# Attention steps spread over a slot, splits at the slot's begin, sample products on GpSimd

## The chip, the cores and the metric

The kernel runs on one core of one Trainium2 chip. Time is device microseconds of one execution; the program is launched once and computes everything in that launch. TensorE is called PE, VectorE DVE, ScalarE ACT, GpSimd POOL and SyncE SP, as in the profile. PEld is the loading of stationary operands on PE.

## The reference, cut to what matters

One layer of a decoder, for a prompt of 2048 tokens and 8 x 4 sample tokens, all in float32. Changed is the scheduling of the first part, the projection and the attention over the prompt:

```python
qa, ka, va, qb, kb, vb, ga, gb = _project(x, w_in)          # one product x @ w_in
qa, ka, qb, kb = _rope(qa, pos), _rope(ka, pos), _rope(qb, pos), _rope(kb, pos)
# A: window of 128, 8 query heads, 2 key heads, a learned sink per head
s = _band_scores(qa.reshape(n, t, A_KV_HEADS, A_GROUP, HEAD_DIM), ka, A_WINDOW)
p = _sink_softmax(s, _sink_logits(sink_a))
oa = _band_values(p, va).reshape(n, t, A_Q)
# B: three groups of 4 heads, (window, dilation) = (128, 1), (512, 4), (2048, 16)
for g, (win, dil) in enumerate(B_DIL):
    qg, kg, vg = (_stride_split(z[:, :, hs], dil) for z in (qb, kb, vb))
    s = _band_scores(qg[:, :, :, None], kg, win // dil)
    p, lse = _softmax_lse(s)
    outs.append(...)                                         # p @ v
```

The scores of a block of 128 queries go against its own block of keys and, where there is one, the block before. The sample tokens attend to caches; the scores of B's sample tokens are sums of products of a query row with cached key rows. After the attention come gates, projections, a layer norm and a gated convolutional FFN, which the change does not touch.

## The kernel before

**Precision.** Every operand of a large product is split into a high and a low half (float32r): `split` copies the high half on ACT and subtracts on DVE (on POOL where it is told so) to get the low half. A product is then three matmuls: high x high, low x high, high x low.

**Slots.** Phase 1 is a row of slots. A slot projects one block of 128 tokens (or the 32 sample tokens) with four units of 256 columns of the weights of its kind. The kinds come in this order: B0, B1, B2 (the three groups of B: q, k, v and a quarter of the gates), A (q, k, v and a part of the gates), G (the rest of the gates). Each has 16 prompt slots; a sample slot, called 16, follows them (in G it comes after the third). A prompt slot is 4 units x 8 k-blocks x 3 = 96 matmuls of 256 columns into two PSUM tiles `psd` (half 0: units 0 and 1, half 1: units 2 and 3; two buffers, so half 0 of the next slot uses the tile of half 0 of this one). The tokens of a slot, `xs`, are split from the transposed input `R` by `make_xs`, one slot ahead; B1 reads R with a stride of 4 tokens, B2 with a stride of 16.

**Steps.** Between groups of 12 matmuls (unit u, half kh of its k-blocks, so eight places a slot, (0, 0) to (3, 1)) `slot` calls `adv`, which advances every attention job by one step (up to its next `yield`). A job is a generator, `attn_b` or `attn_a`, made at a slot's end and advanced through the next slot and into the one after. The order in which Python emits instructions is the order on each engine's queue: an engine takes its instructions strictly in that order, and an instruction that waits holds all those behind it. At (1, 0) and one more place `adv_bg` advances `sample_scores`, which for each pair of sample tokens loads 128 cached keys and the query rows (SP), multiplies them (L797) and sums by head (L800). It gives up four places first, then does 16 pairs: this falls in slots 2 to 9 of B1 and of B2 (two pairs a slot) and 2 to 13 of A (two a slot up to slot 5, then one).

**Evacuation.** When half 0 of psd is complete, `evac` applies the rotary embedding on DVE (`rope`: product with the cosines, product of the swapped halves with the sines, L425 and L426, sum L433); it is emitted at the place `evac_at`. Half 1 is evacuated at the slot's end: the gate's part is copied by ACT (L449); in B the v part stays in PSUM until `split_v` in the job's second step; in A, v is split at once.

**A job of B** transposes q and k (PE), splits them (`split_q`, `split_k`: ACT high, DVE low), computes the scores (`qk`, eight matmuls), and runs the softmax: row maxima with the mask on DVE (L546), minus the scaled maximum `nm` (L550), exponential with the row sum on ACT (L552). P is transposed (PE, L562) and split (`transpose_p`), and multiplied by the values (L659). `both` adds the two halves of the result (ACT L570, DVE L571); POOL adds the parts of two halves (L662) and issues the store (L663). **A job of A** does the same twice, for two head pairs r = 0 and 1 of each key head, with the sink as one more column of P (L693, L695, L698, L700), and stores with two DMAs on POOL (L718).

`bufp` is a ring of ten 2 KB-wide buffers for loads and temporaries. PSUM pools: pd 2 tiles, psS 2 (scores), psT 3 (transposes, and the second of B's value tiles), psO 1.

Of the kernel before, what the change touches and what calls it, by code (L numbers as in the profile page):

```python
# [7 lines left out]
F32 = mybir.dt.float32  # L8
F32R = mybir.dt.float32r
AF = mybir.ActivationFunctionType  # L10
ALU = mybir.AluOpType
# [6 lines left out]
NS = 32  # L18
# [16 lines left out]
class Net:  # L35
# [142 lines left out]
    def phase1(self):  # L178
        nc, tc, a = self.nc, self.tc, self.a
        with ExitStack() as st:  # L180
# [39 lines left out]
            self.jobs = []  # L220
            self.vprev = None
            sa = ExitStack()
            for n, (kind, i, t) in enumerate(seq):
# [16 lines left out]
                def prep():  # L240
# [10 lines left out]
                    if t[0] == "p" and nextp:  # L251
                        return self.make_xs(nextp[0][2], kind == "A")
# [37 lines left out]
    def adv(self):  # L290
        for j in self.jobs[::-1]:
            try:
                next(j)
            except StopIteration:
                self.jobs.remove(j)

# [55 lines left out]
    def slot(self, kind, i, t, xs, units, prep, after_unit, rp):  # L352
# [5 lines left out]
        evac_at = (2, 1) if kind[0] == "B" else (2, 0)  # L358
# [5 lines left out]
        if kind == "A" and i == 16:  # L364
            pace = (0, 0, 1, 1, 1, 1, 2, 2)
        for half in range(2):
            ps = self.pd.tile([128, 512], F32, tag="d", name="psd")
            for uu in range(2):
# [20 lines left out]
                if u == (1 if kind[0] == "B" and i == 0 else 0):  # L389
                    out = prep()  # L390
                    if kind == "G" and i == 14:
                        rp.close()
                        self.phase2_weights()
# [59 lines left out]
    def evac(self, kind, i, t, half, ps):  # L453
# [37 lines left out]
    def evac_sample(self, kind, half, ps):  # L491
# [9 lines left out]
        if half == 0:  # L501
            self.cs_s = self.at.tile([NS, 128], F32, tag="cs", name="css")
            nc.sync.dma_start(self.cs_s, a["c_rope"][rows, :])
            q = self.at1.tile([NS, 512], F32, tag="q", name="sq")
# [36 lines left out]
    def softmax_pair(self, sps, nk, mask, m, nm, den, cols, accum=True, init=None):  # L541
# [8 lines left out]
        nc.vector.tensor_scalar(nm[:, csl], m[:, csl], -SCALE, None, ALU.mult)  # L550
# [71 lines left out]
    def attn_b(self, kind, i, t):  # L622
# [6 lines left out]
        for p in range(2):  # L629
            nc.tensor.transpose(ps[:, p * 128:(p + 1) * 128], q[:, p * 128:(p + 1) * 128], self.idn)  # L630
        qT = self.split_q(ps[:, 0:256].rearrange("p (r t) -> p r t", r=2))
        ps = self.psO.tile([128, 512], F32, tag="o", name="pst")
        for p in range(2):
            nc.tensor.transpose(ps[:, p * 128:(p + 1) * 128], kv[:, p * 128:(p + 1) * 128], self.idn)
# [3 lines left out]
        vprev, self.vprev = self.vprev, v  # L638
        yield
# [4 lines left out]
        nc.gpsimd.dma_start(self.d_md[g, rows, :], md)  # L644
        yield
        vs = [v] if nb == 1 else ([v, vprev] if swap else [vprev, v])
        PTs = []
# [4 lines left out]
        O = self.buf()  # L652
        for x in range(2):
            yield
            ops = self.psT.tile([128, 512], F32, tag="t", name="pso") if x else self.psO.tile([128, 512], F32, tag="o", name="pso")
            for c in range(2):
                for b in range(nb):
                    k = (c * nb + b) * 128
                    nc.tensor.matmul(ops[:, c * 256:(c + 1) * 256], lhsT=vs[b][c][:, x].rearrange("p s d -> p (s d)"),  # L659
                                     rhs=PTs[x][:, :, k:k + 128], start=(b == 0), stop=(b == nb - 1))  # L660
            o = self.both(O, ops, x).rearrange("p (c s t) -> p c s t", c=2, s=2)
# [4 lines left out]
    def attn_a(self, t):  # L666
# [15 lines left out]
        yield  # L682
        m = self.at.tile([128, 8], F32, tag="m8", name="m8")
# [5 lines left out]
        def softmax(r, x, sps):  # L689
# [8 lines left out]
            nc.vector.tensor_scalar(nm[:, c:c + 2], m[:, c:c + 2], -SCALE, None, ALU.mult)  # L698
# [11 lines left out]
        def values(r, x, PT):  # L710
            for b in range(nb):
                for q in range(2):
                    nc.tensor.matmul(ops[:, r * 256:(r + 1) * 256], lhsT=vs[b][:, x], rhs=PT[:, q, b * 256:(b + 1) * 256],
                                     start=(b == 0 and q == 0), stop=(b == nb - 1 and q == 1))

        def out(x):
            o = self.both(O, ops, x)
            nc.gpsimd.dma_start(self.d_oa[x * 256:(x + 1) * 256, rows].rearrange("(h d) t -> d h t", h=4),  # L718
                                o.rearrange("p (h t) -> p h t", h=4))

        sps = scores(0)
        P0, P1 = softmax(0, 0, sps), softmax(0, 1, sps)
        yield
        yield
        t0 = trans(P0)
        sps = scores(1)
        P0 = softmax(1, 0, sps)
        yield
        ops = self.psO.tile([128, 512], F32, tag="o", name="pso")
        values(0, 0, t0)  # L730
        yield
        t0 = trans(P0)
        yield
        P0 = softmax(1, 1, sps)
        yield
        values(1, 0, t0)
        O = self.buf()
        out(0)
        t0 = trans(P1)
        yield  # L740
        t1 = trans(P0)
        yield
        ops = self.psO.tile([128, 512], F32, tag="o", name="pso")
        values(0, 1, t0)
        yield
        values(1, 1, t1)
        out(1)
# [18 lines left out]
    def sample_scores(self, g):  # L766
# [25 lines left out]
        for n, (b, th) in enumerate(steps):  # L792
# [4 lines left out]
            nc.vector.tensor_tensor(q3, Kv, q3, ALU.mult)  # L797
# [835 lines left out]
```

## Time and profile before

| | us |
|---|---|
| median of 3 runs | 3260.72 |
| lowest, highest | 3258.58, 3261.48 |
| the profiled execution | 3259.99 |
| its span, first to last instruction | 3258.2 |
| mean granted clock of TensorE | 0.994 |
| PE busy in the span | 3175.0 |
| DVE busy in the span | 1947.6 |

The span is what the profile shows, and the execution's own time is 1.8 us longer. Phase 1 takes the first 1300 us or so. There the load of the other engines differs from place to place; this is the view that gives each engine's busy time in stretches of 100 us (us of the stretch, then busy us and instructions of each engine, the granted clock, the DMA share and GB/s):

```profile
100.00:200.00 100.00, 100.00 (x856) 99.72 (x856) 62.25 (x164) 61.39 (x155) 17.74 (x26) 1.00 0.17 54
300.00:400.00 100.00, 94.79 (x784) 91.71 (x783) 79.98 (x196) 58.85 (x145) 17.54 (x26) 1.00 0.25 71
600.00:700.00 100.00, 96.80 (x811) 94.57 (x810) 80.23 (x205) 60.28 (x160) 22.70 (x35) 1.00 0.33 99
900.00:1000.00 100.00, 98.27 (x786) 92.55 (x785) 80.11 (x205) 62.37 (x187) 19.11 (x17) 1.00 0.20 50
```

The engines stand in the order PE, PEld, DVE, ACT, POOL. The first stretch lies in B0, the second in B1, the third in B2, the fourth in A. In the rows of groups a line gives: line of the kernel, engine, operation, tiles written and read, shape, count, then busy us in all, mean ns of one, and the idle time of the engine before it with what ended it. In the rows of waits the numbers are us in all, times, and the longest.

### The profile page before, as it was taken

The page shows a single profiled execution, that of the slowest core. Times are in us where ns is not written, and L with a number is a line of the kernel's source. Part 1 is how long each engine was busy: PE and PEld are TensorE (multiplying, and loading weights), DVE is VectorE, ACT ScalarE, POOL GpSimd, SP SyncE. Part 2 cuts the span into 40 slices and gives each one's busy share as a digit, 9 for nine tenths or more (in the row PEclk, how much of TensorE's full clock was granted, in tenths as well). Part 3 has the DMA queues.
Part 4 walks back from the last instruction along what each step waited for, and adds up shares of the span by engine and source line. Part 5 has one row for each costly group of instructions (what it writes and reads, how often), then busy time and mean ns, then how long its engine had stood idle before and what let it go on. Part 6 is the DMA issues. An engine that isn't in the chain of part 4 may idle for free.

```text
span 3258.2 us, 56718 instructions
## 1 busy us (share of the span) xinstructions
PE 3175.0 (97%) x21839; PEld 2907.4 (89%) x21839; DVE 1947.6 (60%) x4030; ACT 1397.0 (43%) x3097; POOL 565.5 (17%) x671
## 2 busy tenths in 40 slices
PE   8999999999999899899999999999999999999999
PEld 8998999999899899788877988888888888999998
DVE  5667877877887632577765444564446444574446
ACT  6666656665666533412224243342243332342332
POOL 2112112223121200255540000030002100030001
PEclk9999999999999999999999999999999999999999
DMA  3113212412221343876744323443334423443231
GB/s 116 56 47 95 82 31 86 121 63 89 79 57 38 91 131 98 227 194 175 187 131 140 121 84 101 127 142 91 95 100 120 139 86 101 120 138 91 69 95 57
DMA packets 480036, 343.02 MB, mean 105 GB/s; under 512 B 113938, under 2 KB 435564, under 8 KB 479766
## 3 DMA queue, kind: packets, MB, share of 16 engines
q1 hardware_dynamic: 462390, 290.78, 31.5%
q0 software_dynamic: 17232, 48.56, 4.8%
q8 instruction: 172, 2.82, 0.4%
q14 instruction: 98, 0.80, 0.1%
q10 hardware_dynamic: 144, 0.07, 0.0%
HBM read 279.71 MB, written 59.59 MB: 104 GB/s over the span
## 4 chain that ended last, share of the span: by engine, by line
PE 58%; issue 2%; DMA 2%; DVE 1%; SPq 0%; ACT 0%; POOL 0%; DVEq 0%; POOLq 0%; ACTq 0%
PE psu L1392 31%; PE psdn L1070 14%; PE psw L1070 5%; PE psb L1070 4%; PE psd L379 2%; PE psdf L1070 1%; DMA oa<-d_oa 1%; PE pst L1234 0%; PE pso L964 0%; PE pst L1269 0%; DMA ob<-d_ob 0%; DMA ga<-d_gate 0%; DMA b<-in_w_o 0%; SPq L1126 0%; DMA b<-in_w_br_b 0%
## 5 line engine op out<-in xcount | busy, mean ns | idle before, releaser
L1392 PE MATMUL psu<-h,w 128*128 128x512 f32 (+1 forms) x5280 | 1013.6, 354 | 2.2 <-ACT h L41 2.0
L379 PE MATMUL psd<-w,xs 128*128 128x256 f32 x7680 | 1001.1, 285 | 8.7 <-ACT w L41 4.0
L1392 PEld LDWEIGHTS psu<-h,w 128*128 128x128 f32 x5280 | 861.2, 188 | 149.0 <-ACT h L41 3.4
L379 PEld LDWEIGHTS psd<-w,xs 128*128 128x128 f32 x7680 | 945.7, 190 | 12.9 <-ACT w L41 4.4
L1070 PE MATMUL psdn<-w,gt 128*128 128x256 f32 (+1 forms) x4008 | 474.9, 279 | 2.2 <-DVE y L1443 2.2
L1070 PEld LDWEIGHTS psdn<-w,gt 128*128 128x128 f32 (+1 forms) x4008 | 472.2, 186 | 5.3 <-DVE y L1443 4.5
L42 DVE TENSOR_TENSOR w<-b,w 128x512 fp32r<-128x512 f32 (+1 forms) x613 | 403.7, 717 | 21.4 <-ACT w L41 20.4
L41 ACT ACTIVATE w<-b 128x512 fp32r<-128x512 f32 x636 | 346.5, 607 | 127.4 <-PE psdn L1070 64.2
L1403 ACT ACTIVATE ext<-psu 128x512 f32<-128x512 f32 (+1 forms) x110 | 56.3, 512 | 452.2 <-PE psu L1392 452.1
L1416 DVE SCALAR_TENSOR_TENSOR ac<-ext,cw,ac 128x512 f32<-128x512 f32 (+1 forms) x88 | 71.1, 808 | 286.9 <-ACT ac L1415 286.9
L1443 DVE SCALAR_TENSOR_TENSOR y<-y,psdn 128x256 f32<-128x256 f32 x176 | 73.2, 420 | 274.2 <-PE psdn L1070 270.4
L1070 PE MATMUL psw<-WO,mT 128*128 128x512 f32 (+1 forms) x800 | 189.4, 395 | 0.9 <-DVE mT L42 0.9
L1070 PEld LDWEIGHTS psw<-WO,mT 128*128 128x128 f32 (+1 forms) x800 | 148.5, 186 | 38.9 <-DVE mT L42 1.1
L1412 POOL COPY mix<-ext 128x2 f32<-128x2 f32 x66 | 13.0, 196 | 926.5 <-ACT ext L1403 906.4
L42 DVE TENSOR_TENSOR xs<-R,xs 128x1024 fp32r<-128x1024 f32 x64 | 104.8, 1638 | 114.9 <-ACT xs L41 114.8
L1070 PE MATMUL psb<-w,oT 128*128 128x512 f32 (+1 forms) x600 | 147.6, 404 | 7.7 <-ACT b L449 5.0
L41 ACT ACTIVATE gt<-ac 128x512 fp32r<-128x512 f32 x110 | 58.3, 549 | 222.2 <-DVE ac L1423 162.7
L1070 PEld LDWEIGHTS psb<-w,oT 128*128 128x128 f32 (+1 forms) x600 | 112.4, 190 | 36.3 <-ACT b L449 5.7
L552 ACT ACTIVATE P<-P,nm 128x256 f32<-128x256 f32 (+1 forms) x192 | 86.4, 451 | 123.1 <-issue 87.4
L42 DVE TENSOR_TENSOR PT<-pst,PT 128x512 fp32r<-128x512 f32 (+1 forms) x160 | 96.2, 608 | 66.6 <-ACT PT L41 66.0
L662 POOL TENSOR_TENSOR b<-b 64x256 f32<-64x256 f32 x96 | 71.3, 742 | 337.4 <-DVE b L571 337.4
L41 ACT ACTIVATE xs<-R 128x1024 fp32r<-128x1024 f32 x80 | 116.2, 1452 | 0.9 <-ACT b L756 0.4
(257 smaller groups left out, 3679.1 us busy)
## 6 DMA issues: line engine op xcount, KB each, us to landing
b<-in_w_up SPq DMA_DIRECT2D x352, 256.0 KB, 3.9
b<-in_w_down SPq DMA_DIRECT2D x160, 256.0 KB, 3.4
b<-in_w_in SPq DMA_DIRECT2D x80, 256.0 KB, 4.1
b<-in_x_prompt SPq DMA_DIRECT2D x64, 256.0 KB, 4.0
b<-in_cache_b SPq DMA_DIRECT2D x64, 256.0 KB, 3.3
ga<-d_gate SPq DMA_DIRECT2D x32, 512.0 KB, 5.4
b<-d_q SPq DMA_DIRECT2D x48, 256.0 KB, 3.9
d_gate<-b SPq DMA_DIRECT2D x64, 128.0 KB, 1.9
```

Of the source, the lines that this page charges most:

```text
L41: self.nc.scalar.activation(hi, src, AF.Copy)
L42: (eng or self.nc.vector).tensor_tensor(lo, src, hi.bitcast(F32), ALU.subtract)
L379: nc.tensor.matmul(dst, lhsT=l, rhs=r[:, k, :], start=(k == 0 and q == 0), stop=(k == 7 and q == len(ops) - 1))
L552: nc.scalar.activation(P[:, x, :nk], P[:, x, :nk], AF.Exp, bias=nm[:, c:c + 1], scale=SCALE, accum_out=den[:, c:c + 1])
L662: nc.gpsimd.tensor_tensor(o[:, :, 0], o[:, :, 0], o[:, :, 1], ALU.add)
L1070: self.nc.tensor.matmul(ps[:x.shape[1]], lhsT=x, rhs=w, start=(first and q == 0), stop=(last and q == len(ops) - 1))
L1392: nc.tensor.matmul(ps[:, :b1 - b0], lhsT=w[:, k, c0:c0 + 128], rhs=h[:, x, k, b0:b1], start=(k == 0 and q == 0), stop=(k == 7 and q == 2))
L1403: nc.scalar.activation(ext[:, 2 + b0:2 + e1], ps[:, 0:e1 - b0], AF.Copy)
L1412: nc.gpsimd.tensor_copy(carry[:, j, :], ext[:, W:W + 2])
L1416: nc.vector.scalar_tensor_tensor(ac[:, :L], ext[:, 1:1 + L], cw[:, 1, j:j + 1], ac[:, :L], ALU.mult, ALU.add)
L1443: nc.vector.scalar_tensor_tensor(y[x][:M, cs], y[x][:M, cs], ALPHA if first else 1.0, ps[:M], ALU.mult, ALU.add)
```

## The change

- **Jobs.** `adv` goes through the jobs from the oldest to the newest (before, the reverse), and then runs what was put on the list `late`.
- **B.** q and k are transposed into one PSUM tile, in one go. The values are split one step later; the scores come one step later. The two transposes of P, before in two separate steps of the same slot, both come at the first place of the next slot, directly ahead of the newer job's transposes. Both value products come together two steps after that, and their sums and store are run from `late`.
- **A.** The scores of r = 0 come one step later with both softmaxes; two steps on both P tiles are transposed, and the scores and both softmaxes of r = 1 follow at once; its transposes come at the first place of the next slot. The values of each r go into one PSUM tile, and each r is stored with two DMAs.
- **xs.** `prep` (loads, the transposes of x in B0, and `make_xs`) is called at the slot's begin, except in B0's first slot. The low half is computed by POOL in B1, B2 and A (before in A alone).
- **rope.** q and k of B lie side by side in one tile, and the rotary embedding takes three DVE instructions for five. Half 0 is evacuated at (2, 0) in B too (before (2, 1)).
- **nm** is computed by ACT.
- **Sample scores.** The product (L797) is done by POOL; the sum stays on DVE.

```diff
     def adv(self):
-        for j in self.jobs[::-1]:
+        for j in list(self.jobs):
             try:
                 next(j)
             except StopIteration:
                 self.jobs.remove(j)
+        while self.late:
+            self.late.pop()()
...
-                        return self.make_xs(nextp[0][2], kind == "A")
+                        return self.make_xs(nextp[0][2], kind != "B0" and kind != "G")
...
-        evac_at = (2, 1) if kind[0] == "B" else (2, 0)
+        evac_at = (2, 0)
...
+        if kind != "B0" or i > 0:
+            out = prep()
...
-            q = self.at1.tile([128, 512], F32, tag="q", name="q")
-            kv = self.at1.tile([128, 512], F32, tag="kv", name="kv")
-            self.q, self.kv = q, kv
+            t = self.at1.tile([128, 1024], F32, tag="qkv", name="qkv")
+            q = t[:, 0:512] if kind == "A" else t[:, 256:512]
+            self.q, self.kv = q, t[:, 512:1024]
...
-                self.rope([(q[:, 0:256].rearrange("p (h d) -> p h d", d=64), 0, 4),
-                           (kv[:, 0:256].rearrange("p (h d) -> p h d", d=64), 4, 8)], ps, cs, 128, 8)
+                self.rope([(t[:, 256:768].rearrange("p (h d) -> p h d", d=64), 0, 8)], ps, cs, 128, 8)
...
-        nc.vector.tensor_scalar(nm[:, csl], m[:, csl], -SCALE, None, ALU.mult)
+        nc.scalar.activation(nm[:, csl], m[:, csl], AF.Copy, scale=-SCALE)
...
 # attn_b
-        for p in range(2):
-            nc.tensor.transpose(ps[:, p * 128:(p + 1) * 128], q[:, p * 128:(p + 1) * 128], self.idn)
+        for p in range(4):
+            nc.tensor.transpose(ps[:, p * 128:(p + 1) * 128], (q, kv)[p // 2][:, p % 2 * 128:(p % 2 + 1) * 128], self.idn)
         qT = self.split_q(ps[:, 0:256].rearrange("p (r t) -> p r t", r=2))
-        ps = self.psO.tile([128, 512], F32, tag="o", name="pst")
-        for p in range(2):
-            nc.tensor.transpose(ps[:, p * 128:(p + 1) * 128], kv[:, p * 128:(p + 1) * 128], self.idn)
-        self.split_k(ps[:, 0:256].rearrange("p (r t) -> p r t", r=2), i % 2)
+        self.split_k(ps[:, 256:512].rearrange("p (r t) -> p r t", r=2), i % 2)
+        yield
         yield
         v = self.split_v(self.vps)
...
         nc.gpsimd.dma_start(self.d_md[g, rows, :], md)
-        yield
...
+        for _ in range(5):
+            yield
+        PTs = [self.transpose_p(P, [(c, b) for c in range(2) for b in range(nb)]) for P in Ps]
+        yield
+        yield
+        tiles = []
         for x in range(2):
-            yield
-            PTs.append(self.transpose_p(Ps[x], [(c, b) for c in range(2) for b in range(nb)]))
...
+        self.late.append(lambda: self.sum_b(g, i, tiles))
+
+    def sum_b(self, g, i, tiles):
+        nc = self.nc
+        O = self.buf()
+        for x, ops in enumerate(tiles):
             o = self.both(O, ops, x).rearrange("p (c s t) -> p c s t", c=2, s=2)
             nc.gpsimd.tensor_tensor(o[:, :, 0], o[:, :, 0], o[:, :, 1], ALU.add)
         nc.gpsimd.dma_start(self.d_ob[g]...)
...
 # attn_a
+        def values(r, PTs):
+            ops = self.psO.tile([128, 512], F32, tag="o", name="pso")
+            for x in range(2):
+                for b in range(nb):
+                    for q in range(2):
+                        nc.tensor.matmul(ops[:, x * 256:(x + 1) * 256], lhsT=vs[b][:, x],
+                                         rhs=PTs[x][:, q, b * 256:(b + 1) * 256],
+                                         start=(b == 0 and q == 0), stop=(b == nb - 1 and q == 1))
+            o = self.both(self.buf(), ops, r)
+            for x in range(2):
+                h0 = (4 * x + 2 * r) * 64
+                nc.gpsimd.dma_start(self.d_oa[h0:h0 + 128, rows].rearrange("(y d) t -> d y t", y=2),
+                                    o[:, x * 256:(x + 1) * 256].rearrange("p (y t) -> p y t", y=2))
...
         sps = scores(0)
+        Ps = [softmax(0, x, sps) for x in range(2)]
+        yield
+        yield
+        PTs = [trans(P) for P in Ps]
         sps = scores(1)
+        Ps = [softmax(1, x, sps) for x in range(2)]
+        yield
+        yield
+        values(0, PTs)
+        yield
+        PTs = [trans(P) for P in Ps]
+        yield
+        yield
+        values(1, PTs)
...
 # sample_scores
-            nc.vector.tensor_tensor(q3, Kv, q3, ALU.mult)
+            nc.gpsimd.tensor_tensor(q3, Kv, q3, ALU.mult)
```

More of the change, by code (lines that the diff above doesn't have):

```diff
@@ L219, in phase1 @@
             units += [self.next_unit(pool=True) for _ in range(2)]
-            self.jobs = []
+            self.jobs, self.late = [], []
             self.vprev = None
@@ L388, in slot @@
                         self.adv_bg()
-                if u == (1 if kind[0] == "B" and i == 0 else 0):
+                if u == 1 and kind == "B0" and i == 0:
                     out = prep()
-                    if kind == "G" and i == 14:
-                        rp.close()
-                        self.phase2_weights()
+                if u == 0 and kind == "G" and i == 14:
+                    rp.close()
+                    self.phase2_weights()
                 after_unit(u)
@@ L503, in evac_sample @@
             nc.sync.dma_start(self.cs_s, a["c_rope"][rows, :])
-            q = self.at1.tile([NS, 512], F32, tag="q", name="sq")
+            q = self.at1.tile([NS, 1024], F32, tag="qkv", name="sq")[:, 0:512]
             kv = self.buf(NS)
@@ L638, in attn_b @@
         vprev, self.vprev = self.vprev, v
+        vs = [v] if nb == 1 else ([v, vprev] if swap else [vprev, v])
         yield
@@ L644, in attn_b @@
         nc.gpsimd.dma_start(self.d_md[g, rows, :], md)
+        for _ in range(5):
+            yield
+        PTs = [self.transpose_p(P, [(c, b) for c in range(2) for b in range(nb)]) for P in Ps]
         yield
-        vs = [v] if nb == 1 else ([v, vprev] if swap else [vprev, v])
-        PTs = []
         yield
+        tiles = []
         for x in range(2):
-            yield
-            PTs.append(self.transpose_p(Ps[x], [(c, b) for c in range(2) for b in range(nb)]))
-        O = self.buf()
-        for x in range(2):
-            yield
             ops = self.psT.tile([128, 512], F32, tag="t", name="pso") if x else self.psO.tile([128, 512], F32, tag="o", name="pso")
+            tiles.append(ops)
             for c in range(2):
@@ L697, in softmax @@
                                                accum_out=m[:, c + y:c + y + 1])
-            nc.vector.tensor_scalar(nm[:, c:c + 2], m[:, c:c + 2], -SCALE, None, ALU.mult)
+            nc.scalar.activation(nm[:, c:c + 2], m[:, c:c + 2], AF.Copy, scale=-SCALE)
             for y in range(2):
@@ L708, in trans @@
             return self.transpose_p(P, [(y, b) for b in range(nb) for y in range(2)])
[L710 to L719, printed above, removed]
+        def values(r, PTs):
[11 more added lines that the diff above has]
+                                    o[:, x * 256:(x + 1) * 256].rearrange("p (y t) -> p y t", y=2))
@@ L721, in attn_a @@
         sps = scores(0)
-        P0, P1 = softmax(0, 0, sps), softmax(0, 1, sps)
+        Ps = [softmax(0, x, sps) for x in range(2)]
         yield
         yield
-        t0 = trans(P0)
+        PTs = [trans(P) for P in Ps]
         sps = scores(1)
-        P0 = softmax(1, 0, sps)
+        Ps = [softmax(1, x, sps) for x in range(2)]
         yield
-        ops = self.psO.tile([128, 512], F32, tag="o", name="pso")
-        values(0, 0, t0)
         yield
-        t0 = trans(P0)
+        values(0, PTs)
@@ L733, in attn_a @@
         yield
-        P0 = softmax(1, 1, sps)
+        PTs = [trans(P) for P in Ps]
         yield
[L736 to L739, printed above, removed]
         yield
[L741 to L747, printed above, removed]
+        values(1, PTs)
     def store_rec(self):
```

## The prediction

> **What bounds the kernel now.** I read the page's busy shares first, then TensorE's (PE's) waits, then the pace of the slots.
>
> ```profile
> PE 3175.0 (97%) x21839; PEld 2907.4 (89%) x21839; DVE 1947.6 (60%) x4030; ACT 1397.0 (43%) x3097; POOL 565.5 (17%) x671
> PE pst L634 <- DVE b L571: 11.7, 19, 0.9
> PE pso L659 <- DVE PT L42: 7.0, 6, 1.9
> PE pso L713 <- DVE PT L42: 6.1, 17, 2.0
> PE pst L562 <- ACT P L552: 4.0, 12, 0.7
> PE psd L379 <- DVE b L426: 3.4, 2, 1.8
> ```
>
> PE bounds the program: 83 us of the span are idle, and the attention's waits, the rows above, are some 32 of them. PE's own work does not change (the same matmuls and transposes), so only stalls can go, or come. The pace of a slot is read from one instruction that occurs once per prompt slot, the high half of xs on ACT; first and last start over one less than the count:
>
> ```profile
> L41 ACT ACTIVATE xs<-R x15: 1060/1064/2072, 34.0 to 249.2; 128x1024 fp32r<-128x1024 f32 x15
> L41 ACT ACTIVATE xs<-R x8: 2062/2069/2078, 310.1 to 420.8; 128x1024 fp32r<-128x1024 f32 x8
> L41 ACT ACTIVATE xs<-R x6: 2025/2070/2100, 435.4 to 511.9; 128x1024 fp32r<-128x1024 f32 x6
> L41 ACT ACTIVATE xs<-R x8: 2002/2008/2026, 572.6 to 673.7; 128x1024 fp32r<-128x1024 f32 x8
> L41 ACT ACTIVATE xs<-R x6: 1065/2004/2021, 688.2 to 759.8; 128x1024 fp32r<-128x1024 f32 x6
> L41 ACT ACTIVATE xs<-R x12: 1061/1064/1066, 818.0 to 1030.3; 128x1024 fp32r<-128x1024 f32 x12
> L41 ACT ACTIVATE xs<-R x2: 1061/1062/1062, 1049.3 to 1068.4; 128x1024 fp32r<-128x1024 f32 x2
> ```
>
> In order: B0 15.4 us a slot; B1 15.8 with sample products (slots 2 to 9) and 15.3 without (10 to 15); B2 14.4 and 14.3; A 19.3 with products (2 to 13) and 19.1 without. Against that stands what PE would need without a stall:
>
> ```profile
> 1273.13 12.11 PE L379 MATMUL psd<-w,xs 128*128 128x256 f32 x101
> 987.85 0.60 PE L562 MATMUL pst<-idn,P 128*128 128x128 f32 x4
> 988.21 1.66 PE L379 MATMUL psd<-w,xs 128*128 128x256 f32 x12
> 989.71 0.60 PE L562 MATMUL pst<-idn,P 128*128 128x128 f32 x4
> ```
>
> 101 matmuls in 12.11 us are 0.118 each, and twelve of them with four transposes take 1.86 (987.85 to 989.71), so a transpose is 0.11, and **a burst has no price of its own**: merging bursts gains nothing by itself. The floors: B0 96 matmuls, 20 transposes, 16 attention matmuls, 15.4; B1 with two key blocks 12 transposes, 14.55; with one block, as all of B2, 13.6; A 21 transposes, 32 attention matmuls, 17.45. So B0 is at its floor, B1 is 0.75 to 1.3 above, B2 0.8, A 1.6 to 1.9.
>
> **The change, part by part.** The rows for it:
>
> ```profile
> L571 DVE TENSOR_TENSOR b<-pso,b 64x512 f32<-64x512 f32 x128 | 87.7, 685 | 24.7 <-ACT b L570 19.9 <-issue 3.6
> L570 ACT ACTIVATE b<-pso 64x512 f32<-64x512 f32 x128 | 75.7, 592 | 70.4 <-PE pso L659 57.5 <-POOL w L42 10.0 <-DVE w L42 1.3
> L662 POOL TENSOR_TENSOR b<-b 64x256 f32<-64x256 f32 x96 | 71.3, 742 | 337.4 <-DVE b L571 337.4
> L663 POOL DMA_DIRECT2D d_ob<-b x48 | 35.2, 732 | 14.3 <-POOL b L662 14.0 <-DVE md L546 0.3
> L718 POOL DMA_DIRECT2D d_oa<-b x32 | 20.2, 633 | 233.8 <-DVE b L571 233.8
> L1063 POOL TENSOR_TENSOR b<-b,gb 128x512 f32<-128x512 f32 x30 | 43.0, 1435 | 1.3 <-DVE b L1060 1.1
> L797 DVE TENSOR_TENSOR b<-b 128x512 f32<-128x512 f32 x48 | 33.0, 688 | 0.1
> L800 DVE TENSOR_REDUCE S<-b 128x8 f32<-128x512 f32 x48 | 33.0, 688 | 1.6
> L695 DVE CUSTOM_DVE_ANT_0 P<-pss,mk,sk 128x256 f32<-128x256 f32 x120 | 52.7, 475 | 0.0
> L546 DVE CUSTOM_DVE_ANT_0 P<-pss,mk 128x256 f32<-128x256 f32 x108 | 41.1, 418 | 0.0
> L700 ACT ACTIVATE P<-P,nm 128x257 f32<-128x257 f32 x120 | 60.3, 504 | 96.8 <-DVE nm L698 96.3
> L41 ACT ACTIVATE PT<-pst 128x512 fp32r<-128x512 f32 x114 | 66.3, 595 | 41.5 <-PE pst L562 40.6
> L604 ACT ACTIVATE kH<-pst 64x256 fp32r<-64x256 f32 x96 | 36.3, 379 | 5.8 <-PE pst L634 3.2
> L604 ACT ACTIVATE kH<-pst 64x128 fp32r<-64x128 f32 x32 | 8.7, 271 | 0.6
> L591 DVE TENSOR_TENSOR qT<-pst,qT 64x256 fp32r<-64x256 f32 x96 | 40.6, 422 | 44.6 <-ACT qT L589 43.2
> L693 ACT ACTIVATE P<-sk 128x2 f32<-128x2 f32 x64 | 12.6, 196 | 0.0
> L449 ACT ACTIVATE b<-psd 128x256 f32<-128x256 f32 x64 | 24.5, 383 | 12.6 <-PE psd L379 6.3 <-DVE vr L443 5.7
> L426 DVE TENSOR_TENSOR b<-psd,cs 128x512 f32<-128x512 f32 x64 | 43.5, 680 | 0.0
> L698 DVE TENSOR_SCALAR nm<-m x48: 168/169/1891, 812.6 to 1039.2; 128x2 f32<-128x2 f32 x48
> L42 POOL TENSOR_TENSOR xs<-R,xs x12: 2386/2394/2407, 819.5 to 1031.5; 128x1024 fp32r<-128x1024 f32 x12
> ```
>
> *xs at the slot's begin, low half on POOL in B1 and B2.* DVE loses some 2.0 us a slot. POOL takes 2.4 by the A rows; R is read there with a stride of 4 or 16, which no POOL row shows, and DVE's own ratio (2.03 against 1.23 in B0) would make it 4. It ends by 7 us, and POOL's next work comes at 9: hidden, unless it took over 6. In B0 both halves merely come earlier. *nm on ACT.* 0.17 leaves DVE, 0.2 joins ACT (as L693, the same size); in A the row's longest 1.89 is an nm that fell into POOL's xs, and that delay goes. The Trainium skill (SBUF — State Buffer, "Who interferes with whom") says the same: such a DVE instruction may need the port pair that GpSimd holds, as may one with two SBUF inputs. By that rule the rope's last add would suffer from more POOL work; the price would be one product's length a slot, where the two meet. *The fourth merged tile (q with k; rope in three instructions)* saves DVE 0.3. *q and k transposed into one PSUM tile*: the wait on L571 at L634 goes. But two engines take turns at one tile even to read it: the gate's copy (L449) waits for DVE's read of vr beside it. So DVE's qT and ACT's kH come one after the other. In us of a B1 slot: gate 0.3 to 0.6, xs 2.07 to 2.65, two PT copies 3.75, two qT 4.5, DVE's two qT rests 0.42 each 5.35, four kH 6.9, DVE's two kL 7.75. B1's scores need kL at 8.2. B2 copies kv first but has half the PT, so kL is as late, and its scores, after less work on PE, want it at 7.25: a stall of 0.5 stays, giving 14.15.
>
> *Spreading.* P is transposed a slot after the scores in B, two groups of twelve after them in A. In B without products the rope has read psd by 12.3 of 14.55: no stall. In A the second P tile is exponentiated at 12.7 (scores at 9.15, two row reductions 0.85, nm 0.2, two exps 1.0, and again nm and exps), PE wants it at 12.3: 0.55 of stall, so 18.0.
>
> *The sample product on POOL.* This is the term that decides. DVE's sum (L800) must now wait for POOL's product, and POOL takes its work in order: the product at (1, 0) stands behind the output of the values that were emitted in the same step. **Behind DVE's waiting sum stand the softmax's row reductions, and in B the rope that frees psd.** Product slot of A, from its first projection matmul: values at 36 x 0.118 + 13 x 0.11 = 5.7 to 6.65, PE's end 6.8. ACT by then: copy of the first values 0.8, DVE's add 1.5 and the k rope's reads 1.9, vr on both 2.55, gate 2.85, xs 3.9, two PT and two qT (0.6 each, the next up to 0.1 early) 6.1, four kH 7.25; so ACT's copy of these values ends at 7.85; DVE's add, after kL (8.1), at 8.8; POOL starts 0.3 after (as before d_ob, 14.0 us over 47), two d_oa of 0.6 to 10.3; product 1.4 (no row for it on POOL; L1063 is the nearest) 11.7; sum 12.4; two row reductions, nm, two exps 14.5. PE wants that tile at 11.8: stall 2.75; the next tile comes at 15.85: stall 0.85. 17.45 + 3.6 = 21.05, against 19.3. Over 12 slots **+21**.
>
> B1: values end at 6.7; vr, which reuses the buffer of the block before the last, waits for them; DVE's two adds, after kL 7.75 and two vr rests 8.25, end at 9.55; POOL's second add 10.4; d_ob 11.4; product 12.85; sum 13.5; four row reductions 14.9; two rope readings 16.25. The next slot's first matmul needs that psd tile: 16.4. With two of eight slots one block (15.3) the mean is 16.1, against 15.8: **+2.5**. B2, with smaller tiles: 15.7 against 14.4, eight slots, **+10**.
>
> split_v, moved a step later, has read psd's second tile by 8.25; PE writes it next at 8.9: nothing, with 0.65 to spare. A issues four d_oa a slot for two (0.6 each on POOL): two are in the chain above, the other two end before xs. POOL's d_md still waits for the exps, with only the second product behind it.
>
> The second product (3, 0) finds DVE and POOL idle at the slot's end: nothing.
>
> *Sum*: products +21, +2.5, +10; B1 without -0.9 x 6 = -5.4; B2 without -0.17 x 6 = -1; A without -1.1 x 2 = -2; B0 none. +25. The turns between kinds, where weights are split on all three engines and xs now comes ahead of them, I bound at -5 and +5 and take nothing. Later phases are untouched.
>
> *The clock.* A slot of A that idles 2.75 and 0.85 us has another price:
>
> ```profile
> 269.84:273.26 3.42, 1.48 (x12) 1.11 (x10) 3.30 (x5) 3.37 (x8) 0.90 (x1) 1.00 0.25 65
> 273.26:276.67 3.41, 3.02 (x14) 2.73 (x13) 3.38 (x8) 0.95 (x2) 1.44 (x2) 0.50 0.48 144
> 286.91:290.32 3.41, 2.16 (x16) 1.95 (x16) 3.38 (x5) 0.40 (x2) 0.13 (x1) 1.00 0.00 0
> ```
>
> PE was busy for 43% of the first window, and the next ran at a granted clock of 0.50; after 63% (the third) it did not fall. 1.7 idle us in 3.4 would do it. A half-clock window costs at most 3.4 / 2 = 1.7, less where it lies over the stall itself. Ends 0 and 1.5 a slot; I take 0.5, since much of it does: +6.
>
> Profiled execution 3260.0 (span 3258.2 and 1.8 around it), 0.7 under the median: 3260 + 25 + 6 = **3291**.
>
> **The rivals.** *(a) Faster: DVE's relief decides.* If POOL had the product done before DVE comes to the sum, every slot falls to its floor: 16 product slots of B and 12 of A lose no more (8 x -1.5, 8 x -0.3, 12 x -1.3, with the -8 above): -38, 3222. For it: DVE loses 2.7 to 3.4 us in a product slot. Against it: POOL's order; it decides from the point where the product ends before DVE's second add, at 8.8 in A, and it starts later. *(b) The clock falls in every A slot*, 12 x 1.5 = 18 for 6: 3303. The Trainium skill (TensorE: Matmul & The Clock Gate, "The HAM clock gate") wants a whole idle window of about 3.4 us; by it a 2.75 us stall costs no clock, and the time would be 3285. The first window above, idle for 57%, speaks against the page. *(c) The chains are 1.2 us shorter than I add them up*, each hand-over a little quicker than a full duration: 28 x 1.2 = 34 less, 3257, no change.
>
> **Chances.** Forecast 0.50, (a) 0.20, (b) 0.15, (c) 0.15 with a quarter of it below. Under 0.2% (6.5 us) this kernel's runs cannot tell a difference. Faster 0.24, same 0.09, slower 0.67. The range leaves out most of (a): 3238 (between (c) and (a)) to 3308 ((b) with +5 at the turns).
>
> **What would show it.** Product slots of A at about 21 us, with PE waiting for ACT's P (L562) some 2.7 us, DVE's sum (L800) waiting for POOL's product, the nm on ACT at 0.2; B product slots with L379 waiting for L426; L634's wait gone; B0 at 15.4. Wrong would be: DVE's sum seldom waiting, A slots under 18.5, or transposes that cost less in a long burst.

## The result and the profile after

The changed kernel takes **3305.04 us** (median; 3261.1 before, on the same chip): a ratio of 1.0135, 95% interval 1.0115 to 1.0154. The median counts a fourth execution, a slow one of 7240.67 us; the ratio is taken from the other three (3303.4 to 3306.07). Its profiled execution has a span of 3301.6 us against 3258.2, so 43.4 us have to be found. They lie in the attention over the prompt, in the slots with a sample product.

The page's busy time and the first of TensorE's waits in the changed kernel (us in total, times, longest):

```profile
PE 3186.0 (96%) x21839; PEld 2931.2 (89%) x21839; DVE 1808.3 (55%) x3694; ACT 1419.0 (43%) x3257; POOL 747.5 (23%) x783
```

```profile
PE pst L565 <- ACT P L708: 29.4, 40, 2.0
PE psd L383 <- DVE b L430: 26.3, 18, 2.1
```

VectorE (DVE) lost 139 us of work, GpSimd (POOL) got 182, and the kernel is slower: what engines do in total does not decide here. The wait of the k transposes on the output add (11.7 us before) is gone from the list. In its place TensorE waits for the exponential in A (L708) and for the rope's reading of psd in B (L430; 3.4 us before). Before, the exponential in A (there L700) held it for 1.5 us in all.

The pace of the slots, again from the high half of xs on ScalarE, whose place is now the slot's begin. In order (B0 keeps its pace, 43.2 to 242.0 over 13): B1 with products (slots 2 to 9, and the start of 10); B1 without; B2 with, B2 without, A with (2 to 13), and the end of A:

```profile
L41 ACT ACTIVATE xs<-R x9: 2058/2081/2094, 303.7 to 438.0; 128x1024 fp32r<-128x1024 f32 x9
L41 ACT ACTIVATE xs<-R x6: 1980/2070/2076, 438.0 to 508.9; 128x1024 fp32r<-128x1024 f32 x6
L41 ACT ACTIVATE xs<-R x9: 1975/1999/2018, 569.8 to 696.3; 128x1024 fp32r<-128x1024 f32 x9
L41 ACT ACTIVATE xs<-R x5: 1974/1995/1997, 696.3 to 751.3; 128x1024 fp32r<-128x1024 f32 x5
L41 ACT ACTIVATE xs<-R x12: 1052/1055/1058, 828.5 to 1071.5; 128x1024 fp32r<-128x1024 f32 x12
L41 ACT ACTIVATE xs<-R x3: 1052/1055/1057, 1071.5 to 1111.5; 128x1024 fp32r<-128x1024 f32 x3
```

Last start less first, over one less than the count, beside the paces that the prediction read of before:

| slots | before | forecast | after | over all such slots |
|---|---|---|---|---|
| B0 | 15.4 | 15.4 | 15.3 | 0 |
| B1 with products (8) | 15.8 | 16.1 | 16.8 | +8 |
| B1 without (6) | 15.3 | 14.4 | 14.2 | -7 |
| B2 with products (8) | 14.4 | 15.7 | 15.8 | +11 |
| B2 without (6) | 14.3 | 14.15 | 13.75 | -3 |
| A with products (12) | 19.3 | 21.05 and 0.5 of clock | 22.1 | +34 |
| A without (2) | 19.1 | 18.0 | 18.0 | -2 |

(The last row: from 1071.5 to 1111.5 there are one slot with a product, 22, and one without.) The sum is +41; the other 2 us of the span are in the turns between kinds and the phases behind.

One slot of A in the timeline of the changed kernel, from its first projection matmul at 957.47 (start, duration, engine, line, and in brackets the idle time before and what ended it):

```profile
963.15 1.11 PE L723 MATMUL pso<-PT,vr 128*128 128x256 f32 x8
...
964.61 0.59 ACT L573 ACTIVATE b<-pso 64x512 f32<-64x512 f32 x1
...
965.39 0.69 DVE L574 TENSOR_TENSOR b<-pso,b 64x512 f32<-64x512 f32 x1
...
966.37 1.22 POOL L729 DMA_DIRECT2D d_oa<-b  x2 [2.51 <-DVE b L574]
966.53 3.00 PE L383 MATMUL psd<-w,xs 128*128 128x256 f32 x24
967.62 1.30 POOL L796 TENSOR_TENSOR b<-b 128x512 f32<-128x512 f32 x1
968.95 0.69 DVE L799 TENSOR_REDUCE S<-b 128x8 f32<-128x512 f32 x1 [2.88 <-POOL b L796]
969.67 0.48 DVE L703 CUSTOM_DVE_ANT_0 P<-pss,mk,sk 128x256 f32<-128x256 f32 x1
...
970.60 0.20 ACT L706 ACTIVATE nm<-m 128x2 f32<-128x2 f32 x1 [5.17 <-DVE m L703]
...
971.49 0.33 PE L565 MATMUL pst<-idn,P 128*128 128x128 f32 x1 [1.97 <-ACT P L708]
```

The scores are there at 966.7, the product's inputs long before. Yet POOL first starts the two transfers of the output, then makes the product, and VectorE stands for 2.88 us at the sum with the softmax of finished scores behind it. Values, copy, add, two transfers, product, sum, softmax: they run one behind the other over four engines, each in the order of its queue. Over the program VectorE waits so 44 times of 48:

```profile
DVE S L799 <- POOL b L796: 123.2, 44, 3.9
```

Then comes what the stall does to the clock. Windows of 3.41 us of the same kernel; behind each engine's busy us is its count of instructions, and the number after POOL's is TensorE's granted clock:

```profile
857.91:861.32 3.41, 1.76 (x15) 1.56 (x14) 2.17 (x8) 0.52 (x2) 2.40 (x2) 1.00 0.10 19
861.32:864.74 3.42, 2.48 (x16) 1.86 (x17) 3.36 (x8) 3.23 (x13) 0.00 (x0) 1.00 0.00 0
970.56:973.97 3.41, 1.87 (x11) 1.26 (x12) 2.91 (x10) 3.14 (x13) 0.00 (x0) 1.00 0.01 2
973.97:977.39 3.42, 3.42 (x19) 3.42 (x18) 2.87 (x10) 1.85 (x8) 0.00 (x0) 0.50 0.00 0
825.00:1090.00 265.00, 235.87 (x1783) 224.44 (x1782) 155.90 (x412) 149.09 (x469) 78.97 (x76) 0.93 0.20 52
```

The first two windows, with 15 and 16 TensorE instructions, were each followed by one at 1.00. The window that holds the end of the stall and the short waits behind it (970.56) has 11, and the next, on the same grid, runs at 0.50. Over the whole stretch of A the clock is 0.93: 0.07 of 265 us is 18.6, eleven windows at half clock, nearly one for each product slot.

### The profile page after: what moved, and what is told of

It reads as the page before. It is cut to its first block, busy times and chain, and to the rows that moved or that the text cites. A ratio compares the mean times of both kernels' runs of the same rounds, so it can differ in the third digit from the quotient of the medians.

```text
span 3301.6 us, 56714 instructions
## 1 busy us (share of the span) xinstructions
PE 3186.0 (96%) x21839; PEld 2931.2 (89%) x21839; DVE 1808.3 (55%) x3694; ACT 1419.0 (43%) x3257; POOL 747.5 (23%) x783
## 4 chain that ended last, share of the span: by engine, by line
PE 63%; issue 6%; DVE 4%; ACT 3%; POOL 2%; DMA 2%; SPq 0%; DVEq 0%; POOLq 0%; ACTq 0%
PE psu L1391 30%; PE psdn L1069 14%; PE psd L383 6%; PE psw L1069 4%; PE psb L1069 3%; PE psdf L1069 1%; ACT P L708 1%; PE pst L565 1%; DMA oa<-d_oa 1%; PE pso L723 1%; DVE b L574 1%; POOL b L796 0%; PE pss L622 0%; PE pss L620 0%; ACT qT L592 0%
## 5 line engine op out<-in xcount | busy, mean ns | idle before, releaser
L383 PE MATMUL psd<-w,xs 128*128 128x256 f32 x7680 | 988.4, 286 | 40.9 <-DVE b L430 26.3
L42 POOL TENSOR_TENSOR xs<-R,xs 128x1024 fp32r<-128x1024 f32 x48 | 132.5, 2761 | 51.6 <-ACT xs L41 37.3
L565 PE MATMUL pst<-idn,P 128*128 128x128 f32 x548 | 91.3, 298 | 30.4 <-ACT P L708 29.4
L42 DVE TENSOR_TENSOR xs<-R,xs 128x1024 fp32r<-128x1024 f32 x32 | 41.6, 1299 | 142.7 <-ACT xs L41 142.6
```

Source lines behind the costliest of these rows:

```text
L42: (eng or self.nc.vector).tensor_tensor(lo, src, hi.bitcast(F32), ALU.subtract)
L383: nc.tensor.matmul(dst, lhsT=l, rhs=r[:, k, :], start=(k == 0 and q == 0), stop=(k == 7 and q == len(ops) - 1))
L565: nc.tensor.transpose(ps[:, n * 128:(n + 1) * 128], P[:, x, b * 128:(b + 1) * 128], self.idn)
```

## The experiments

Times are read against the kernel before on the same chip (3262.97, 3258.94, 3258.64 and 3262.38 us in the four sets below, in order of the labels 1 to 4, 5 to 8, 9 and 10, 11 and 12). Labels e6, e10 and e11 were executed four times each and have intervals; the others are one execution each, good to some 4 us, since the kernel before itself ranged from 3256.15 to 3263.71.

### The product alone, both ways

```
# e1_product_dve: the changed kernel
-            nc.gpsimd.tensor_tensor(q3, Kv, q3, ALU.mult)
+            nc.vector.tensor_tensor(q3, Kv, q3, ALU.mult)
# e2_before_product_pool: the kernel before
-            nc.vector.tensor_tensor(q3, Kv, q3, ALU.mult)
+            nc.gpsimd.tensor_tensor(q3, Kv, q3, ALU.mult)
```

> The changed kernel with the sample product back on DVE, all else as changed. Theory (DVE's sum waits in its queue for POOL's product and holds softmax and rope): product slots of A fall from 22.1 to 18.1 to 18.6 us, those of B1 from 16.8 to 14.6, of B2 from 15.8 to 13.8; 12 x 3.8 + 8 x 2.2 + 8 x 2.0 = 79 less, 3226 us. Rival 1 (a busier POOL slows DVE at the port they share, xs above all): 3290 to 3305, since xs stays on POOL. Rival 2 (the spread of the attention over a slot makes the stalls): 3300 to 3305.

> The kernel before with the sample product on POOL and nothing else. Theory: there too the product stands on POOL behind a DMA that waits for the softmax (d_md in B, the output in A), and DVE's sum behind it holds the split of P and the rope: 1 to 2 us more in each of the 28 product slots, 3285 to 3310 us. Rival 1: POOL has room in that kernel, at most 5 us more. Rival 2: no change, 3260.

e1 took 3234.75 us, 28 less than the kernel before: this one line turns the sign of the whole change. TensorE's wait for the exponential in A went from 29.4 us in total to 7.0, the longest from 2.0 to 0.3. e1 missed its 3226 in A, where a slot takes 19.1 us (xs from 793.5 to 1003.9 over 11) and not 18.1 to 18.6: product and sum, 0.69 us each, now stand on VectorE ahead of the softmax. e2 took 3295.59, 33 more than the kernel before, with nothing else changed. TensorE's first two waits in it:

```profile
PE pso L659 <- DVE PT L42: 21.6, 22, 2.5
PE psd L379 <- DVE b L426: 14.8, 18, 1.4
```

They are VectorE's copies of P and its rope, both behind a sum that waits. But in e2 the loss is all in B; its A slots keep 19.5 us (xs from 849.4 to 1063.5, 11 slots), which I had not expected. VectorE's sum waits for the product 16 times in all, 8 in B1 and 8 in B2; in A it never does:

```profile
DVE S L800 <- POOL b L797: 56.6, 16, 5.2
```

So the move is no loss by itself where the product is done before VectorE comes to the sum. Then order should decide, which the next two ask.

### Order on GpSimd's queue

```
# e3_product_first: the changed kernel; the product's step is called ahead of the attention's step
+                    if (u, kh) == (1, 0):
+                        self.adv_bg()
                     self.adv()
...
# e4_store_after_product: the changed kernel; in A the two transfers of the slot's second half
# (values of r = 1) are issued behind the product
```

> The changed kernel with the step of the sample scores at (1, 0) emitted ahead of the attention's step instead of behind it; POOL does the same work in another order. Theory: the product stands right behind xs on POOL, done at 7.8 us of an A slot, and DVE has its sum behind it before the values are there: slots as in the run with the product on DVE or a little shorter, 3218 to 3228 us. Rival 1 (POOL's work as such): 3300 to 3305. Rival 2: 3300 to 3305.

> The changed kernel with the two output DMAs of A's second values issued behind the sample product instead of ahead of it (A alone). The product starts 1.2 us earlier. By the chain alone each of A's 12 product slots gets 1.2 us shorter, 3290 us. By the chain with the clock (the stall then is some 1.0 and 0.9 us, and no window is idle by half) the half-clock windows in A go too, another 1.0 a slot: 3278 us.

e3 took 3236.55: the earlier place of the product brings nearly all of the gain, and A runs at 18.3 us (801.8 to 1003.4 over 11). It missed its 3218 to 3228 in B, where the product now starts behind GpSimd's xs, and the sum with it holds VectorE's vr (the low half of v):

```profile
PE psd L383 <- DVE vr L449: 5.2, 14, 0.5
```

e4 took 3262.58. Its slots of A ran at 18.2 us (830.5 to 1030.6 over 11) for 22.1; B stayed as in the changed kernel. POOL in a slot of A that begins at 936.59:

```profile
940.70 2.40 POOL L42 TENSOR_TENSOR xs<-R,xs 128x1024 fp32r<-128x1024 f32 x1 [0.99 <-ACT xs L41]
943.06 1.28 POOL L805 TENSOR_TENSOR b<-b 128x512 f32<-128x512 f32 x1
945.60 1.25 POOL L733 DMA_DIRECT2D d_oa<-b  x2 [1.26 <-DVE b L576]
```

The expected gain (to 3278 or 3290) was too small: I had the product late only by the transfers' own 1.2 us, but a transfer at the head of the queue also holds it until VectorE's add is done. Put ahead of the transfers, the product follows xs and is finished 7.75 us after the slot's begin instead of 11.45 (968.92 in the timeline above). Not one instruction less: 44 us (43.9 over the kernel before, and now 0.4 under it) for the order of two entries in one queue.

### What the clock adds

```
# e5_fill: the changed kernel, ahead of the transposes of A's first P tiles
+        if 1 <= i <= 12:
+            fill = self.psT.tile([128, 512], F32, tag="t", name="fill")
+            for _ in range(16):
+                nc.tensor.matmul(fill[:, 0:nk], lhsT=qT[0][:, 0], rhs=self.kH[0][:, 0, sl, :], start=True, stop=True)
```

> The changed kernel with work added: 16 dummy matmuls of the scores' shape, into a scratch PSUM tile that nobody reads, stand on TensorE ahead of the transposes of the first P tile in twelve slots of A, where TensorE waits for the exponential (some 2 us a slot). Theory: nearly every product slot of A has a window of 3.41 us at a granted clock of 0.50, because TensorE idles 3.4 us of a slot; with the wait filled no window falls, and a product slot of A takes 20.9 to 21.2 us for the 22.1 of the changed kernel, the whole about 3291 us: less time with more work. Rival: the half-clock windows lie over waiting and cost nothing; then 3305, or as much more as the filling itself delays (up to 12 x 1 us).

It took 3289.72 us: 192 matmuls more, and 30.8 over its kernel before where the changed kernel was 43.9 over its own; 13 us less. The window over the same slots:

```profile
825.00:1078.00 253.00, 244.68 (x1980) 233.07 (x1980) 155.04 (x412) 149.25 (x470) 79.05 (x76) 1.00 0.21 54
```

No half clock is left (1.00), and a slot takes 21.0 us (xs from 828.4 to 1059.7, over 11) for 22.1. The stall itself is still there, only covered: VectorE's wait for the product is 123.1 us, as in the changed kernel. So of A's +34, the clock's share is 13 (12 x 1.1), and that of the wait 21. The granted clock alone would make the share 18.6; what covers the rest, no run shows.

### VectorE need not wait

```
# e6_sum_later: the changed kernel; the sum is put on a list and emitted later
-            nc.vector.tensor_reduce(...)
+            self.sums.append(lambda c0=c0, qb=qb: total(c0, qb))
...
+                    if (u, kh) in ((0, 1), (2, 0)):      # e10_sum_once: == (2, 0)
+                        while self.sums:
+                            self.sums.pop(0)()
```

> The changed kernel, its product on GpSimd as it is, but VectorE's sum over the product emitted one or two steps later, behind the slot's softmax and rope, so that VectorE never waits for GpSimd's product. Theory (VectorE's wait in order of its queue is the loss): product slots go to about 14.5 in B1, 13.7 in B2, 18.0 to 18.3 in A, the whole 3222 us (3214 to 3228). Rival 1 (a busier GpSimd costs as such, through the port or the buffers): 3280 to 3305, A slots over 20. Rival 2 (the spread of the attention costs): 3295 to 3305.

> As e6_sum_later, but with both sums of a slot emitted at one place, after the slot's softmax and rope; in e6_sum_later the sum over the second product of the slot before still stood between VectorE's kL and its vr or output add, and held TensorE 0.45 us in B2 (psd waiting for VectorE's vr). Theory (each sum costs what stands behind it on VectorE): B2 product slots 14.4 to 13.7 (8 x 0.65), some of the same in B1 and in A's slots 3 to 6 (19.2 to 18.5): 3231 less 6 to 10, so 3221 to 3226. Rival: the rope's last add, 1.65 us for 0.69 where GpSimd's product runs beside it, is what holds these slots; then 3229 to 3233.

e6 took 3231.4 us, a ratio of 0.9916 (0.9899 to 0.9932); e10 **3224.0**, 0.9893 (0.9877 to 0.991). The product is on GpSimd in both, as in the changed kernel: the wait, not the engine, cost the 79 us between e10 (34.6 under its kernel before) and the changed kernel (43.9 over its own). VectorE's wait for the product is gone from e10's list. B2 and A of e10:

```profile
L41 ACT ACTIVATE xs<-R x9: 1975/1987/2000, 550.2 to 660.0; 128x1024 fp32r<-128x1024 f32 x9
L41 ACT ACTIVATE xs<-R x12: 1052/1054/1057, 790.4 to 991.6; 128x1024 fp32r<-128x1024 f32 x12
```

13.7 a slot and 18.3. e6 missed its expectation (3222) because one of its two sums still stood ahead of VectorE's vr, which TensorE wants; e10 moved that one and came in where it was expected. Its rival, the longer rope add, is real but falls where nobody waits. VectorE's last add of the rope in B2, which takes 0.69 us in the changed kernel (L437, nine of them within 0.01), in e10:

```profile
L440 DVE TENSOR_TENSOR qkv<-qkv,b x8: 1628/1694/1703, 560.8 to 656.9; 128x512 f32<-128x512 f32 x8
```

In e10 it runs beside GpSimd's product and is held 1.0 us in every slot. The slots stand within 0.1 us of their floor all the same.

### What the moves off VectorE are worth

```
# e7_nm_dve: e6 with nm on VectorE, in B and in A
-        nc.scalar.activation(nm[:, csl], m[:, csl], AF.Copy, scale=-SCALE)
+        nc.vector.tensor_scalar(nm[:, csl], m[:, csl], -SCALE, None, ALU.mult)
# e8_xs_dve: e6 with the low half of xs on VectorE in B1 and B2, still at the slot's begin
-                        return self.make_xs(nextp[0][2], kind != "B0" and kind != "G")
+                        return self.make_xs(nextp[0][2], kind == "A")
```

> As e6_sum_later, with the negated row maximum nm on VectorE again, in A and in B. If the collision of a 128x2 nm with GpSimd's long instruction (1.89 us for 0.17 in the kernel before) recurs, GpSimd's product and xs in A will catch some of the nm, and a product slot of A takes 1 us more: 3230 to 3236. If nm on ScalarE has no value of its own: as e6_sum_later within 3 us.

> As e6_sum_later, with the low half of xs on VectorE again in B1 and B2 (2 us a slot on VectorE, as before the change). Where VectorE's relief in B is worth nothing by itself once the products are gone from it: as e6_sum_later within 3 us. Where the 2 us keep k and the rope late: B1 slots 15.0 or more, B2 slots 14.0 or more, 8 to 20 us above e6_sum_later.

e7 took 3257.9 us, 26 more than e6. VectorE's nm in A of e7, and one of them with what GpSimd does beside it:

```profile
L709 DVE TENSOR_SCALAR nm<-m x56: 169/169/3123, 792.3 to 1058.4; 128x2 f32<-128x2 f32 x56
```

```profile
915.55 1.41 DVE L709 TENSOR_SCALAR nm<-m 128x2 f32<-128x2 f32 x1
915.63 1.29 POOL L803 TENSOR_TENSOR b<-b 128x512 f32<-128x512 f32 x1
```

An instruction of 0.17 us ends when GpSimd's ends, and up to 3.12 us pass where two products follow each other. The softmax waits for it: a slot of A takes 20.2 us (822.3 to 1044.8 over 11) where e6 has 18.3 (799.8 to 1001.6). I had taken one collision of 1 us in each of A's 12 product slots, and no pairs.

e8 took 3292.95, 62 more than e6, where I had at most 20. Here the slot's begin hurts too: VectorE reaches its half of xs first, waits for ScalarE's half, and holds everything else. VectorE in a slot of B2 without products, begun at 739.32:

```profile
742.08 1.97 DVE L42 TENSOR_TENSOR xs<-R,xs 128x1024 fp32r<-128x1024 f32 x1 [5.91 <-ACT xs L41]
743.98 0.73 DVE L42 TENSOR_TENSOR PT<-pst,PT 128x256 fp32r<-128x256 f32 x2
```

The copies of P begin 4.7 us into the slot, and q, k and the scores after them. TensorE then works so thinly that its clock falls, in a slot with a product begun at 721.93:

```profile
728.79:732.20 3.41, 2.46 (x14) 1.69 (x13) 2.26 (x6) 2.63 (x7) 0.00 (x0) 1.00 0.00 0
732.20:735.62 3.42, 3.42 (x17) 3.42 (x18) 3.32 (x13) 1.70 (x9) 2.18 (x3) 0.51 0.00 0
```

So two of the change's edits seem to hang together: xs can stand at the slot's begin since its low half is on GpSimd. That is read from these rows; no run has the changed attention with VectorE's half of xs at its old place.

```
# e9_relief_only: the kernel before, attention as it was, product on VectorE
-                        return self.make_xs(nextp[0][2], kind == "A")
+                        return self.make_xs(nextp[0][2], kind != "B0" and kind != "G")
-        nc.vector.tensor_scalar(nm[:, csl], m[:, csl], -SCALE, None, ALU.mult)
+        nc.scalar.activation(nm[:, csl], m[:, csl], AF.Copy, scale=-SCALE)
# e12_nm_only: the second edit alone (both places of nm)
```

> The kernel before with only two of the moves: the low half of xs on GpSimd in B1 and B2 as well (at its old place, after the first quarter of the slot), and the negated maximum nm on ScalarE. No spread attention, no merged transposes, the sample product on VectorE as before. If relief of VectorE alone makes the gain seen where the product holds nobody: about 3235 us, B slots without products at 14.6 and 13.7, A slots at 18.0. If the spread of the attention is needed for it: 3243 to 3250, B slots 0.3 to 0.7 us above their floors, A slots 18.3 to 18.8, and the waits on ScalarE's copies stay.

> The kernel before with nm on ScalarE alone (xs in B on VectorE as before): parts the gain of e9_relief_only (35 us) between its two moves. Theory (in A, nm on VectorE waits out GpSimd's xs): A slots go from 19.0 to 18.0, those with two products from 19.7 to 18.3, B unchanged within 0.2 a slot: 13 x 1.0 + 4 x 0.4 = 15, so 3242 to 3246. Rival (nm is only short work taken off VectorE): A slots 18.6 or more, 3253 to 3257.

e9 took 3223.85 us, e12 3248.7. The slots of A take 18.1 us in both: in e9 199.1 over 11 (xs from 798.2 to 997.3), in e12 199.0 (819.8 to 1018.8).

A's gain is nm's alone: e12 is 14 us under its kernel before (I had 15). The low half of xs on GpSimd gives the other 21, in B. e9 beat my expectation for it (3235 at best): no spread of the attention is needed for the gain, and e9 and e10, which differ in all the rest of the change, are equal within what one execution can tell. In e9 xs on GpSimd has its collision too, with VectorE's product of two SBUF inputs, 0.69 us by itself; the rows are of B1:

```profile
340.12 2.90 POOL L42 TENSOR_TENSOR xs<-R,xs 128x1024 fp32r<-128x1024 f32 x1
340.60 2.98 DVE L797 TENSOR_TENSOR b<-b 128x512 f32<-128x512 f32 x1
```

### Both together

```
# e11_relief_product: e9, and the product on GpSimd with its sums emitted after the slot's rope
+                    if (u, kh) == (2, 1):
+                        while self.sums:
+                            self.sums.pop(0)()
-            nc.vector.tensor_tensor(q3, Kv, q3, ALU.mult)
+            nc.gpsimd.tensor_tensor(q3, Kv, q3, ALU.mult)
```

> e9_relief_only (3223.85) and the sample product on GpSimd too, with its sums on VectorE emitted after the slot's rope; attention as in the kernel before. Theory (VectorE's work is worth moving wherever VectorE doesn't wait for the result): the product no longer stands between VectorE's softmax, rope and output adds, B1 product slots go from 15.37 to 14.6, B2 ones from 14.13 to 13.6, A unchanged at 18.0 to 18.4: 3223.9 less 6 to 10, so 3214 to 3219. Rival (GpSimd with its xs, output add, stores and product in one slot is now itself late, and a longer collision with VectorE's two-input adds takes the gain back): 3222 to 3235.

3224.92 us, a ratio of 0.9886 (0.9869 to 0.9904): no gain over e9, as the rival has it. B1's product slots take 14.8 us for e9's 15.0, but B2's 14.4 for 14.1; there the k transposes wait for the output add 5.1 us in all, for 2.4 in e9. One reason that the rows show is the rival's collision. VectorE's rope add for q in B2, first in e9, then in e11, where GpSimd's products run beside it in all eight product slots:

```profile
L433 DVE TENSOR_TENSOR q<-q,b x9: 424/425/428, 566.5 to 679.4; 128x256 f32<-128x256 f32 x9
L436 DVE TENSOR_TENSOR q<-q,b x9: 426/755/1559, 565.2 to 680.9; 128x256 f32<-128x256 f32 x9
```

The other is the place of the sums. The slot's end in B2 of e11:

```profile
609.98 1.27 DVE L793 TENSOR_REDUCE S<-b 128x8 f32<-128x512 f32 x2
...
611.50 0.67 DVE L574 TENSOR_TENSOR b<-pso,b 64x512 f32<-64x512 f32 x1
...
612.23 0.44 PE L637 MATMUL pst<-idn,kv 128*128 128x128 f32 x2 [0.49 <-DVE b L574]
```

I had put the two sums (1.27 us) behind the rope, and in this kernel's order that is just ahead of the output add for which the k transposes wait. In e9 the second product and its sum stand there, 0.68 and 0.69 us, so nothing is relieved. An earlier place, where VectorE idles (4.1 us before the copies of P in that slot), was not tried.

## Why the prediction was right, point by point

The forecast was 3291 us, slower; measured 3305.04, inside the range, near its upper end. That is the number of rival (b), 3303, in part by luck: it has all of its 12 us from the clock in A, and of the 14 us over the forecast about 7 are that and 5.5 are B1's.

- **The deciding term was the right one.** The product stands behind the output work, VectorE's sum waits, the softmax and the rope wait behind it. In the slot shown, 957.47 and the steps' 7.85, 8.8, 10.3, 11.7 and 12.4 stand against 7.73 (ACT's copy ended), 8.61, 10.12, 11.45 and 12.17: every link within 0.25 us. Forecast for A was +21 without the clock; e5, where the clock is taken out, has +21. The stalls on TensorE that I made it of were too long, though: 1.97 us for 2.75 in the slot shown, and 29.4 in all for 12 x 3.6. How the rest of the +21 is spread, no row shows. B2: +10 forecast, +11 measured.
- **The clock was mis-sized.** I took 0.5 us a slot of A between ends of 0 and 1.5, +6; e5 puts it at 1.1 a slot, 13. That it would fall was read rightly from two windows of before. The step that failed is that much of a half-clock window would lie over the stall itself, for which I had no row: in the slot shown it begins at 973.97, the long stall had ended at 971.49, and it lies over work without a gap (3.42 busy us of 3.42). The Trainium skill (TensorE: Matmul & The Clock Gate, "The HAM clock gate") asks for a whole idle window of some 3.4 us. The trace does not agree: the window before the fall had 1.87 busy us. By that rule the forecast would have been 3285.
- **B1 with products was mis-sized**, +2.5 for +8. In the chain to kL I left out that VectorE's two rests of PT stand ahead of its rests of q (the second row waits for them in turn):

```profile
339.39 1.29 DVE L42 TENSOR_TENSOR PT<-pst,PT 128x512 fp32r<-128x512 f32 x2
...
340.71 0.87 DVE L594 TENSOR_TENSOR qT<-pst,qT 64x256 fp32r<-64x256 f32 x2
...
341.62 0.77 ACT L607 ACTIVATE kH<-pst 64x256 fp32r<-64x256 f32 x2 [1.14 <-DVE qT L594]
```

The slot began at 335.80: VectorE's q is done 5.78 after it where I had 5.35, and all links behind are 0.5 late, so that psd comes free 16.8 after the begin, not 16.25. Three windows of B1 at half clock come on top, one of them from 386.88 to 390.30, at 0.50, behind this window:

```profile
383.47:386.88 3.41, 1.33 (x12) 1.15 (x11) 3.03 (x11) 2.87 (x12) 0.09 (x1) 1.00 0.00 0
```

- **The slots without products** went as forecast (A 18.0; B1 14.2 for 14.4). In B2 the expected half microsecond at the scores did not come (13.75, the floor is 13.6). That q and k, now in one PSUM tile, are read in turns was right: the kH row above waits for VectorE's qT. What it costs is under 0.2 us a slot.
- **xs hidden on GpSimd, nm on ScalarE**: right. That bursts of transposes gain nothing fits too: e9, without them, is as fast as e10, with them.
- **Rival (a), 3222**, was the right price for the wrong order: e4 (in A), e6 and e10 are what it describes, and e10 measures 3224. Its stated point held: the product must not stand behind the output.
- **Rival (c)** fell: the links were not 1.2 us shorter.

What stays open: how the 2 us in the turns between kinds and the phases behind come about, and how far e9 and e10 differ, since e9 has no interval.

## What to carry to other kernels

An operation moved to an idle engine is paid for by whoever consumes it: before the move, list what stands ahead of it on its new queue and what stands behind the instruction that will wait for it. Here the order of two transfers, or a sum emitted later in the slot, turned +44 us into 0 and into -35. Idle time of some 2 us on TensorE must be priced with the clock that follows it, here another 1.1 us a slot.

## What the runs showed of the hardware

- **The clock falls after a thin window, not only after an idle one.** TensorE's windows lie on a grid of 3.41 us: each window of that length quoted here has a clock of 0.50, 0.51 or 1.00, none a value between. Of those quoted, the ones with 11 and 12 TensorE instructions were followed by a window at half clock, those with 15 and 16 were not; 14 did both, in e8 above and, with the next window (29 instructions) at 1.00, here in the changed kernel:

```profile
332.27:335.68 3.41, 1.59 (x14) 1.38 (x12) 3.36 (x11) 1.82 (x8) 0.00 (x0) 1.00 0.01 2
```

From 270 to 1095 us of the changed kernel all sixteen windows at full clock with 5 to 12 instructions were followed by one at half clock, and none with 14 or more; in e8 some with 14, 16 and 17 were. The busy us sort them worse (2.46 fell, 1.59 did not); the ends of matmuls are modelled.

- **A short VectorE instruction can be held for the whole of a GpSimd one**: nm, 0.17 us, took up to 3.12; a two-input add of 0.69 took 1.69, a product of 0.69 took 2.98. The Trainium skill (SBUF — State Buffer, "Who interferes with whom") names both kinds, and the runs agree on that. ScalarE's nm took at most 0.21 in the changed kernel and in e10, there also inside a pair of GpSimd's products (798.46 to 798.65, the products 797.21 to 799.76).
